# Weight residuals of thirteen units: ScalarE and an accumulating transfer in place of a VectorE subtraction

## The chip, the cores and the metric

One core of a Trainium2 chip runs the kernel. The metric is the device time of one execution in microseconds (us), and less is better. The engines named below are TensorE (PE in the profile), VectorE (DVE), ScalarE (ACT), GpSimd (POOL) and SyncE (SP), which here only issues transfers. TensorE's clock has two levels, 1.2 and 2.4 GHz; the profile gives the granted clock as a share of the upper one.

## What is computed

A decoder trunk of two layers over 512 tokens of width 1024, in float32. Each layer normalizes its input, multiplies it by one combined matrix, and splits the columns among two mixers: a diagonal state space model (S5) and a gated linear attention (GLA). Their outputs go through one output matrix and are added to the input; then a SwiGLU feed-forward block is added.

```python
for i in range(DEPTH):
    z = rmsnorm(x, norm_mix[i]) @ w_in[i]          # u | q | k | v | g | gate
    y = gelu(s5(u)); y = y * sigmoid(y @ w_glu[i] + b_glu[i])
    x = x + concat([rmsnorm(y), gla(q, k, v, g, gate)]) @ w_out[i]
    gu = rmsnorm(x, norm_ffn[i]) @ w_ffn_in[i]
    x = x + (silu(gu[..., :D_FF]) * gu[..., D_FF:]) @ w_ffn_out[i]
return rmsnorm(x, norm_final)
```

## The kernel before, in words

Activations lie transposed, features on the 128 partitions and the 512 tokens along the free axis. Each large matrix product is made three times to keep float32 accuracy: weights and activations are both split into a rounded part (`hi`, type float32r) and the residual that rounding leaves (`lo`), and `mm3` (L575 to L578) adds up hi times hi, hi times lo and lo times hi. L576 and L577 need only the rounded weights (`whi`), L578 needs the residuals (`wlo`).

The weights are cut into 128x128 blocks in the order in which they are used, and eight blocks make a unit of 512 KB (`UB = 8`). The first layer's units are: 0 to 3 the columns u, 4 to 7 q, k, q, k, 8 to 10 three tiles of g, 11 to 14 the columns v, 15 the last tile of g, 16 and 17 the `glu` matrix, 18 and on the output matrix and the feed-forward block. The class `Weights` brings them in:

- `load` (L142) has SyncE issue the transfer of one unit from HBM into a `raw` tile. There are two `raw` buffers, so the load of unit v+2 waits until nothing reads raw unit v any more.
- `ensure` (L155 to L168) prepares units up to two ahead of the one in use. For each it issues the next load, has ScalarE round raw into `whi` (L163), and has VectorE subtract, raw minus `whi`, into `wlo` (L165); unit 17's subtraction is made by GpSimd instead (`POOL_W`). There are three buffers each of `whi` and `wlo`, so the rounding of unit v waits for TensorE to be done with unit v-3.

What sets the order: TensorE, ScalarE and SyncE work in the order in which the program is written (`manual_schedule`), and so does VectorE in the first layer up to unit 10. GpSimd's order, and VectorE's elsewhere, is written by a planner ahead of the run from times that it assumes; the subtraction has high priority in it. Every engine then works strictly through its queue, so an instruction that waits holds all that is behind it.

Beside the products of units 3 to 15 the first layer also prepares its S5 mixer. `prep_w` builds the matrix `Wk`: VectorE transposes 128x512 tiles (L441), and for each of eight tiles SyncE issues four small transfers into `Wk` (`place`, L446), in the same queue as the loads of raw weights. `prep_v` and `prep_rot` build `Vx`, `Tz`, `cosT` and `sinT` on GpSimd (L407 to L417, L567 to L572). Then, for each of four groups b, `s5_fwd(b)` multiplies U by `Wk` (L833), VectorE rotates (L841 to L844), GpSimd adds (L846, L847), VectorE scans (L852); `s5_back(b)` rotates back on VectorE and GpSimd (L866 to L874); `s5_y(b)` is TensorE's product of the result (L888, L890) and ScalarE's gelu (L899). These calls are spread over the products of v by `v_tiles`. After them come `y_split` (L583, L584), the last tile of g (L992, L1001) and `glu`.

Of the kernel before, what the change touches and what calls it, by code (L numbers as in the profile page):

```python
# [10 lines left out]
F32 = mybir.dt.float32  # L11
# [3 lines left out]
ALU = mybir.AluOpType  # L15
# [24 lines left out]
GLU_MID = 1  # L40
NORM_AT = 3
RF_AT = 4
POOL_W = (17,)
FF_PARTS = (3, 4, 5, 5, 5)

O_Q, O_K, O_V, O_G, O_R = 512, 768, 1024, 1536, 2048
# [81 lines left out]
class Weights:  # L128
# [27 lines left out]
    def ensure(self, u):  # L156
        while self.next_split <= min(u + self.LOOK, DEPTH * NUNIT - 1):
            v = self.next_split
            self.load(v + 1)
            raw = self.raw.pop(v)  # L160
            hi = self.pool.tile([P, UB * P], F32R, tag="whi", name=f"whi{v}", bufs=3)
            lo = self.pool.tile([P, UB * P], F32R, tag="wlo", name=f"wlo{v}", bufs=3)
            self.nc.scalar.copy(hi, raw)  # L163
            with self.tc.high_priority():
                (self.nc.gpsimd if v in POOL_W else self.nc.vector).tensor_tensor(lo, raw, hi.bitcast(F32), op=ALU.subtract)  # L165
            self.split[v] = (hi, lo)
            self.next_split += 1
            self.split.pop(v - 6, None)  # L168
# [1341 lines left out]
```

## Time and profile before

| | |
|---|---|
| median of three runs | 1160.06 us (1159.01 to 1160.10) |
| the profiled execution | 1159.86 us |
| its span, first to last instruction | 1158.1 us |
| mean granted TensorE clock | 0.987 |
| TensorE busy | 1110.1 us, 96% of the span |
| VectorE busy | 706.2 us, 61% |
| ScalarE busy | 485.6 us, 42% |
| GpSimd busy | 331.9 us, 29% |
| the rounding L163 | 183 times, 1050 ns each |
| VectorE's subtraction L165 | 182 times, 1333 ns each |
| load of a raw unit | 183 times, 512 KB, 3.5 us to landing (median) |

The shares are means over the whole span. Over most of it, the feed-forward blocks and the second layer, TensorE has hardly a gap. The units that the change touches are used in the first 190 us, and that stretch is read by itself, from tables of ten microseconds each, the engines' own timelines and the waits.

### The profile page before, as it was taken

The numbers are of one execution on the slowest core, as the hardware profiler recorded it, in microseconds if no ns is written. First come the engines' busy times: TensorE is split into PE (matmuls) and PEld (weight loads), VectorE is DVE, ScalarE is ACT, GpSimd is POOL, SyncE is SP. The second block draws the span as 40 slices with busy tenths as digits, with TensorE's granted clock in tenths as the row PEclk, the third lists the DMA queues.
The fourth block names the chain that finished last, engine by engine and source line by source line (L and its number), as shares of the span: only waits on it lengthen the run. The fifth ranks groups of instructions, "written<-read, shape, count | busy, mean of one in ns | idle before, by whom it ended". The sixth has DMA issues, their size and how long they took to land.

```text
span 1158.1 us, 13973 instructions
## 1 busy us (share of the span) xinstructions
PE 1110.1 (96%) x5316; PEld 913.9 (79%) x5316; DVE 706.2 (61%) x947; ACT 485.6 (42%) x844; POOL 331.9 (29%) x322
## 2 busy tenths in 40 slices
PE   8789779999999999999999799999999999999997
PEld 5568658888888888888887688888888888888886
DVE  7996976866454454564466994686545444444454
ACT  6853458443232232432358653745323222222243
POOL 6899544546000052065030440352000000000003
PEclk9899889999999999999999999999999999999999
DMA  6155111244343523232331212123332333223221
GB/s 211 55 112 126 37 37 37 92 130 116 103 109 100 137 91 101 82 109 91 93 104 41 73 61 85 56 91 94 107 100 85 106 99 102 91 91 109 91 91 73
DMA packets 64099, 107.72 MB, mean 93 GB/s; under 512 B 37408, under 2 KB 38304, under 8 KB 64032
## 3 DMA queue, kind: packets, MB, share of 16 engines
q1 hardware_dynamic: 63888, 106.56, 30.2%
q8 instruction: 42, 0.69, 0.2%
q10 hardware_dynamic: 144, 0.26, 0.1%
q14 instruction: 25, 0.20, 0.1%
HBM read 100.52 MB, written 2.10 MB: 89 GB/s over the span
## 4 chain that ended last, share of the span: by engine, by line
PE 79%; DVE 12%; ACT 3%; issue 2%; POOL 2%; DMA 1%; SPq 1%; DVEq 0%; POOLq 0%; ACTq 0%
PE fg L576 7%; PE fg L577 7%; PE fg L578 7%; PE fu L578 7%; PE fu L576 7%; PE fu L577 7%; PE fo L578 7%; PE fo L576 7%; PE fo L577 7%; DVE ro L852 2%; DVE wlo L165 2%; ACT U L745 1%; DVE qz L814 1%; DMA wrr<-in_wr_dram 1%; DMA raw<-in_wst_dram 1%
## 5 line engine op out<-in xcount | busy, mean ns | idle before, releaser
L165 DVE TENSOR_TENSOR wlo<-raw,whi 128x1024 fp32r<-128x1024 f32 x182 | 242.2, 1333 | 113.2 <-ACT whi L163 112.0
L163 ACT CAST whi<-raw 128x1024 fp32r<-128x1024 f32 x183 | 191.8, 1050 | 280.0 <-PE fo L577 116.9
L602 POOL TENSOR_TENSOR sq_fin<-sq_fin 128x512 f32<-128x512 f32 x5 | 6.5, 1296 | 341.8 <-ACT sq_fin L598 341.8
L1237 DVE TENSOR_TENSOR fu<-fu,rs_ffn 128x512 f32<-128x512 f32 x44 | 30.4, 691 | 116.7 <-PE fu L578 113.9
L1254 DVE TENSOR_TENSOR xall<-xall,fo 128x512 f32<-128x512 f32 x78 | 53.1, 686 | 61.9 <-PE fo L578 61.7
L1234 DVE TENSOR_TENSOR fg<-fg,rs_ffn 128x512 f32<-128x512 f32 x44 | 30.3, 688 | 34.7 <-PE fg L578 30.8
L1236 ACT ACTIVATE fg<-fg 128x512 f32<-128x512 f32 x44 | 27.7, 629 | 42.5 <-DVE fg L1234 42.4
L899 ACT ACTIVATE y<-y 32x128 f32<-32x128 f32 x128 | 34.4, 269 | 20.9 <-PE y L890 17.3
L1238 DVE TENSOR_TENSOR fu<-fg,fu 128x512 f32<-128x512 f32 x44 | 31.3, 711 | 5.7 <-ACT fg L1236 1.3
L745 ACT COPY U<-u 32x128 f32<-32x128 f32 x128 | 32.9, 257 | 1.5
L852 DVE TENSOR_TENSOR_SCAN ro<-sp_mag,ro 128x128 f32<-128x128 f32 x64 | 28.5, 507 | 6.6 <-POOL ro L846 6.6
L1089 POOL TENSOR_TENSOR xall<-xall,wo 128x512 f32<-128x512 f32 x16 | 25.5, 1613 | 24.0 <-DVE wo L1088 24.0
L407 POOL TENSOR_TENSOR pt<-bc,sp_a1r 128x256 f32<-128x256 f32 x2 | 1.7, 852 | 94.0 <-issue 92.0
L568 POOL TENSOR_TENSOR rt<-rg 128x512 f32<-128x512 f32 x8 | 10.2, 1288 | 59.8 <-ACT rg L548 59.7
L602 POOL TENSOR_TENSOR sq_s<-sq_s,sq_s 128x512 f32<-128x512 f32 x6 | 8.1, 1342 | 64.3 <-ACT sq_s L598 64.3
L869 POOL TENSOR_TENSOR sr<-ro,ro 128x508 f32<-128x508 f32 x8 | 14.6, 1826 | 39.3 <-DVE ro L867 39.3
L602 POOL TENSOR_TENSOR sq_x1nmix<-sq_x1nmix 128x512 f32<-128x512 f32 x7 | 9.2, 1315 | 57.3 <-ACT sq_x1nmix L598 57.3
L890 PE MATMUL y<-sr,Vx 128*128 128x128 f32 x64 | 15.0, 322 | 8.0 <-POOL sr L869 7.8
L890 PE MATMUL y<-sm,Vx 128*128 128x128 f32 x64 | 14.8, 318 | 6.2 <-POOL sm L874 6.2
L888 PE MATMUL y<-U,Tz 128*128 128x128 f32 x64 | 14.9, 320 | 5.5 <-DVE ro L842 5.4
L846 POOL TENSOR_TENSOR ro<-ro,ro 128x512 f32<-128x512 f32 x8 | 10.7, 1344 | 30.8 <-DVE ro L843 30.8
L890 PEld LDWEIGHTS y<-sr,Vx 128*128 128x128 f32 x64 | 11.9, 231 | 8.9 <-POOL sr L869 8.9
(1257 smaller groups left out, 3533.0 us busy)
## 6 DMA issues: line engine op xcount, KB each, us to landing
raw<-in_wst_dram SPq DMA_DIRECT2D x183, 512.0 KB, 3.5
Wk<-wt SPq DMA_DIRECT2D x64, 64.0 KB, 3.9
xall<-in_xt_dram SPq DMA_DIRECT2D x3, 512.0 KB, 8.5
out_dram<-fin SPq DMA_DIRECT2D x6, 256.0 KB, 2.2
bc<-in_s5bc_dram SPq DMA_DIRECT2D x4, 256.0 KB, 4.1
raw<-in_wst_dram SPq DMA_DIRECT2D x1, 384.0 KB, 5.8
cst<-in_const_dram SPq DMA_DIRECT2D x1, 384.0 KB, 5.0
xall<-in_xt_dram SPq DMA_DIRECT2D x1, 283.0 KB, 3.0
```

The source lines that it names most:

```text
L163: self.nc.scalar.copy(hi, raw)
L165: (self.nc.gpsimd if v in POOL_W else self.nc.vector).tensor_tensor(lo, raw, hi.bitcast(F32), op=ALU.subtract)
L576: nc.tensor.matmul(ps, whi, xh, start=start, stop=False)
L577: nc.tensor.matmul(ps, whi, xl, start=False, stop=False)
L578: nc.tensor.matmul(ps, wlo, xh, start=False, stop=stop)
L745: nc.scalar.copy(u[32 * t:32 * t + 32, j].rearrange("p (n c) -> p n c", n=NCH), pv[32 * j:32 * j + 32, :, t, :],)
L852: v.tensor_tensor_scan(dst[:, cs], sp["mag4"][:, c:c + 1].to_broadcast([P, P]), src[:, cs], 0.0, M, A)
L890: nc.tensor.matmul(o, Vx[:, pr, part, 1:].rearrange("p a b c -> p (a b c)"), s_[:, cs], start=False, stop=(part == 1),)
L899: nc.scalar.activation(yv[32 * j:32 * j + 32, :, t, :], ps[32 * t:32 * t + 32, j * P:(j + 1) * P].rearrange("p (n c) -> p n c", n=NCH), AF ...
L1237: nc.vector.tensor_tensor(u, pu, rstd[0], op=M)
L1238: nc.vector.tensor_tensor(u, g, u, op=M)
L1254: nc.vector.tensor_tensor(xT[n], xT[n], ps[n], op=A)
```

## The change

For the first layer's units 5 to 17, ScalarE writes the negated rounded weights into `wlo` with a second instruction, and then GpSimd issues a transfer from `raw` to `wlo` that adds what it carries to what is there, so that `wlo` ends as raw minus hi. The subtraction on VectorE (units 5 to 16) and on GpSimd (unit 17) is gone. The transfer has the high priority that the subtraction had. All other units stay as they were.

```diff
-POOL_W = (17,)
+POOL_W = ()
+DMA_W = range(5, 18)
...
             self.nc.scalar.copy(hi, raw)
-            with self.tc.high_priority():
-                (self.nc.gpsimd if v in POOL_W else self.nc.vector).tensor_tensor(lo, raw, hi.bitcast(F32), op=ALU.subtract)
+            if v in DMA_W:
+                self.nc.scalar.mul(lo, hi.bitcast(F32), -1.0)
+                with self.tc.high_priority():
+                    self.nc.gpsimd.dma_start(lo.bitcast(F32), raw, accum_op=ALU.add)
+            else:
+                with self.tc.high_priority():
+                    (self.nc.gpsimd if v in POOL_W else self.nc.vector).tensor_tensor(lo, raw, hi.bitcast(F32), op=ALU.subtract)
             self.split[v] = (hi, lo)
```

## Rows read from the trace of the kernel before

**Rows 1.** Table by stage: stretch, length, busy us (instructions) by engine, clock, DMA, GB/s.

```profile
10.00:20.00 10.00, 8.56 (x35) 6.03 (x35) 9.49 (x8) 6.97 (x13) 5.86 (x4) 1.00 0.89 312
...
50.00:60.00 10.00, 9.45 (x42) 7.49 (x40) 9.86 (x10) 9.77 (x25) 9.85 (x12) 1.00 0.25 96
...
80.00:90.00 10.00, 10.00 (x48) 8.29 (x47) 9.89 (x12) 2.10 (x2) 9.71 (x9) 1.00 0.82 161
90.00:100.00 10.00, 10.00 (x51) 8.33 (x50) 5.84 (x8) 3.94 (x6) 10.00 (x8) 1.00 1.01 226
...
120.00:130.00 10.00, 4.97 (x21) 4.70 (x22) 9.80 (x20) 2.75 (x4) 7.08 (x8) 0.67 0.17 52
```

**Rows 2.** TensorE's timeline: start us, length us, what [idle before <-releaser].

```profile
62.38 0.79 PE L578 MATMUL q<-x0h,wlo 128*128 128x512 f32 x1 [2.93 <-DVE wlo L165]
...
71.14 0.50 PE L578 MATMUL k<-x0h,wlo 128*128 128x512 f32 x1 [1.68 <-DVE wlo L165]
...
101.47 1.13 PE L833 MATMUL x<-U,Wk 128*128 128x128 f32 x8 [1.00 <-DMA Wk<-wt]
...
118.30 0.39 PE L915 MATMUL v<-whi,x5l 128*128 128x512 f32 x1
...
124.07 0.76 PE L888 MATMUL y<-U,Tz 128*128 128x128 f32 x2 [5.38 <-DVE ro L842]
...
130.41 1.95 PE L833 MATMUL x<-U,Wk 128*128 128x128 f32 x16
```

**Rows 3.** Rounding and subtraction, 0 to 250 us: duration ns min/median/max, first and last start.

```profile
L163 ACT CAST whi<-raw x30: 1029/1046/1077, 10.7 to 246.9; 128x1024 fp32r<-128x1024 f32 x30
...
L165 DVE TENSOR_TENSOR wlo<-raw,whi x29: 1176/1314/2136, 11.8 to 248.2; 128x1024 fp32r<-128x1024 f32 x29
...
L165 POOL TENSOR_TENSOR wlo<-raw,whi x1: 2382/2382/2382, 160.2 to 160.2; 128x1024 fp32r<-128x1024 f32 x1
```

**Rows 4.** ScalarE's timeline: the roundings of units 6 and 7.

```profile
55.53 1.05 ACT L163 CAST whi<-raw 128x1024 fp32r<-128x1024 f32 x1
...
67.03 1.05 ACT L163 CAST whi<-raw 128x1024 fp32r<-128x1024 f32 x1
```

**Rows 5.** SyncE's timeline: issues of raw loads and of transfers into Wk.

```profile
67.36 4.08 SPq L142 DMA_DIRECT2D raw<-in_wst_dram  x2
...
96.01 2.71 SPq L446 DMA_DIRECT2D Wk<-wt  x4
```

**Rows 6.** Issues of raw loads, 55 to 105 us, and their time to landing.

```profile
L142 SPq DMA_DIRECT2D raw<-in_wst_dram x8: 333/560/1301, 67.4 to 99.3; - x8
...
DMA to landing us min/median/max: 3.5/4.3/5.2
```

**Rows 7.** Time to landing of all raw loads of the run.

```profile
DMA to landing us min/median/max: 2.8/3.5/7.7
```

**Rows 8.** GpSimd's timeline.

```profile
83.88 1.24 POOL L567 TENSOR_TENSOR cosT<-rk 128x512 f32<-128x512 f32 x1
85.08 2.04 POOL L570 TENSOR_TENSOR sinT<-rg,rk 128x512 f32<-128x512 f32 x1
...
112.49 1.29 POOL L846 TENSOR_TENSOR ro<-ro,ro 128x512 f32<-128x512 f32 x1
...
160.16 2.38 POOL L165 TENSOR_TENSOR wlo<-raw,whi 128x1024 fp32r<-128x1024 f32 x1
```

**Rows 9.** VectorE's timeline.

```profile
84.87 1.33 DVE L165 TENSOR_TENSOR wlo<-raw,whi 128x1024 fp32r<-128x1024 f32 x1
...
133.96 1.21 DVE L165 TENSOR_TENSOR wlo<-raw,whi 128x1024 fp32r<-128x1024 f32 x1
135.20 0.69 DVE L841 TENSOR_TENSOR ro<-x,cosT 128x512 f32<-128x512 f32 x1
...
160.24 2.85 DVE L584 TENSOR_TENSOR yg01l<-y,yg01h 128x512 fp32r<-128x512 f32 x1
```

**Rows 10.** Waits between 40 and 190 us: who for whom, us in total, times, longest.

```profile
PE gl L576 <- ACT yg03h L583: 3.0, 1, 3.0
```

## The prediction

> **What bounds the kernel now.** Read the table by stage first, and of it only the first 190 us; after that TensorE runs without a gap, so what the change gains or loses on the way to there arrives at the end one for one. From 50 us on VectorE and GpSimd are both busy for some 99% of the time [rows 1]. VectorE has less to do from 90 us; GpSimd stays full to about 118 us. The DMA engines are busy for 0.82 and 1.01 of 80 to 100 us [rows 1], mostly with the small transfers into Wk. Next, TensorE's timeline shows what is late. Twice it stands before a residual: 2.93 us for unit 6 and 1.68 us for unit 7 [rows 2]. At 101.47 it stands for Wk, and from 118.7, when v's sixth step ends, it stands 5.38 us for the first S5 product [rows 2]. After that wait the granted clock of the stretch is 0.67 [rows 1]: the product and its surroundings take from 124.07 to 130.41, where the lower level of 1.2 GHz, in place of 2.4, costs about half. The S5 group that TensorE waits for hung on GpSimd: L846 starts at 112.49, behind the preparation [rows 8], and VectorE's scans come after it. So three things end last in turn: VectorE's queue (to 80 us), GpSimd's preparation (to 118 us), and the exchange of VectorE and GpSimd (to 165 us).
>
> **What is removed.** Twelve subtractions on VectorE, 1.31 us each [rows 3], 15.8 us; and one of 2.38 us on GpSimd. Those of units 6 to 14 (nine) lie beside GpSimd's preparation and slow it: L570 took 2.04 us beside the subtraction of 84.87, L567, of the same shape, 1.24 just before [rows 8, 9]. At 0.8 us each GpSimd would get back up to 7 us; I take 4, since other VectorE instructions move into the place of some. Units 15 and 16 lie in the exchange, where VectorE's next instruction comes directly behind (133.96 to 135.20) [rows 9]; without them the exchange is 2 x 1.2 = 2.4 us shorter. Unit 17's subtraction on GpSimd, 160.16 to 162.54 [rows 8], lies beside VectorE's L584, which took 2.85 us [rows 9], though the same shape takes about 0.7 elsewhere on that engine (L841 [rows 9]). That L584 stands ahead of the last g tile, the last gelu and y3's split, for which TensorE waits 3.0 us [rows 10]. So 2.85 - 0.7 = 2.1 us come back there, and this I count as gained in every case.
>
> **What is added on ScalarE.** A second instruction of the rounding's shape, 1.05 us [rows 3], per unit. ScalarE is full from 40 to 67 us (9.77 of 10 us in 50:60 [rows 1]), so the negations of units 5 and 6 delay the work behind them, the roundings of later units included. Unit 6 is rounded at 55.53 + 1.05 = 56.6 and negated by 58.7; unit 7 is rounded at 67.03 + 2.1 = 69.1 and negated by 71.2 [rows 4]. Later ScalarE waits for loads, and the negation lengthens that path alone.
>
> **What is added on GpSimd, the queue and the buffer.** No row of this run shows a transfer issued by GpSimd or an adding one, so its price D, from the end of the negation to the residual in place, is bounded. It has three parts. Waiting for GpSimd's running instruction: 0 to a whole one of 1.24 us [rows 8], half of it, 0.6, taken. Issuing: between SyncE's shortest issue in this stretch, 0.33 us [rows 6], and GpSimd's whole 128x1024 subtraction, 2.4 us [rows 8]; I take 1.0, nearer to the issue, since no elements are computed. Moving: a raw load of the same 512 KB lands in 4.3 us here [rows 6], between 2.8 and 7.7 over the run [rows 7]. At 312 GB/s and 0.89 busy [rows 1] the engines would move 350 GB/s, so 0.524 MB are 1.5 us of their time. The adding transfer reads two tiles, so I take 4.3 + 1.5 = 5.8 us. A gain from D itself is excluded: a transfer can't land before it is issued. Sum D = 0.6 + 1.0 + 5.8 = 7.4; low end 0 + 0.3 + 2.8 = 3.1; high end 1.2 + 2.4 + 7.7 = 11.3.
>
> D matters because raw is held until the transfer has landed. SyncE's load of unit v+2 waits for it, and behind that load in SyncE's queue are the transfers into Wk, which alternate with the loads [rows 5]. The negations of units 6 and 7 end at 58.7 and 71.2, so their residuals are there at 66.1 and 78.6, where TensorE had them at 62.4 and 71.1 [rows 2]. From then on a round is load 4.3, rounding and negating 2.1, D 7.4, some 14 us for two units; TensorE's own work for two units is 11 (24 products of 0.227 us each). By the odd units: load 9 at 78.7, residual 9 at 92.5, residual 11 at 106.4. By the even ones: load 8 at 67.4 [rows 5], residual 8 at 81.1, load 10 at 81.8 (behind four Wk transfers that waited behind load 9), residual 10 at 95.6, load 12 at 95.8, residual 12 at 109.6, load 14 at 109.8. The last four Wk transfers start at 110.4 where they started at 96.01 [rows 5]: 14.4 us late, three times D and a constant.
>
> **What of that reaches the end.** TensorE's wait at 101.47 ends at 115.9, and it comes to the first S5 product at 118.7 + 14.4 = 133.1 in place of 124.07: 9.0 us late. It comes there straight from work, so the product runs at the upper level and takes about half of 6.3 us, 3.1 less; against that, it now stops some 4 us for Wk (v's first step, held by residual 11 until 106.4, ends 5.5 later), which by the 3.1 us that the stop of 5.4 cost in its wake I put at 2 us of lower level behind it. The third group's input (130.41 before [rows 2]) starts 9.0 - 3.1 + 2.0 = 7.9 us late, at 138.3, and ends at 140.2, where VectorE took it up at 135.2 [rows 9]: 5.0 us late. VectorE itself, which has lost the subtractions of 15 and 16, would have been there earlier. From there the exchange runs as before, 5.0 late. GpSimd's nine issues (9 x 1.0 - 4 = 5 us later at L846, 117.5) stay under it: 117.5 - 112.5 - 2.4 = 2.6. Together 5.0 - 2.1 = **+2.9 us**. By one us of D this moves by 3 in the range in which the round trip is the bound, which ends at about D = 5.5 below.
>
> On the profiled execution (1159.86, 1.76 us more than its span) that is 1162.8; on the median of the runs, 0.2 us higher, **1163.0**. About 0.2%, 2.3 us, is what a measurement of this kernel can tell from no change.
>
> **Rivals.** (a) *The transfer is quick and VectorE's relief wins.* For it: SBUF to SBUF has no HBM in its way, and the shortest load lands in 2.8 us [rows 7]. Below D of some 5.5 Wk is late by less than TensorE's stop at 124 covers, and the exchange is 2.4 us shorter, the split 2.1: up to -4.5, 1155.6; at D = 5.5 some -2.8. Middle 1156.5. Against it: the DMA engines are full at 80 to 100 us [rows 1], and eight more transfers of two reads each, 3 us of engine time each, come into that stretch. The Trainium skill's page "DMA: Bandwidth & Descriptors", section "Anatomy of one DMA — SWDGE (gpsimd) path", puts such a transfer at 2.0 us plus its bytes at 436 GB/s; an estimate by it is 3.2 us for one tile, D would be near 4 to 5, and the time about this rival's. No run here shows that figure yet.
>
> (b) *GpSimd becomes the bound by its order.* Its queue was written ahead; a transfer placed there waits for a negation that waits for a load that waits for an earlier transfer, and cosT, sinT, Tz and L846 stand behind it. That GpSimd has no gap between 46 and 118 us now (9.85, 9.71 and 10.00 us of 10 [rows 1]) is the case for it: each stop goes to L846. It decides once stops and issues together exceed the 5 us that I have counted by more than 2; nine transfers at 2 us each would be 18 - 4 = 14 late at L846, less 2.4 and 2.1: +9.5, **1169.6**. Against it: with the priority that it has the planner puts it where it believes the negation done.
>
> (c) *All is hidden.* Wk and the residual are late by just what the stop at 124 and the quicker exchange give back: within 2 us, 1160.
>
> That the change doesn't do what it says would be VectorE still making twelve subtractions; nothing points to it.
>
> **How the numbers follow.** Forecast (D of 6 to 9, -1.3 to +7.7) 0.40, of it 0.14 within 0.2%, 0.24 slower, 0.02 faster; (a) 0.28, of it 0.26 faster; (b) 0.20, slower; (c) 0.12, same. Sums: faster 0.28, same 0.28, slower 0.44. The range leaves out 0.1 on either side: below at the quick end of (a), 1155.5; above at D near 11.3, +2.9 + 3 x 3.9 = +14.6, and most of (b): 1174.7. The likeliest case's own range is 1158.8 to 1167.8.
>
> **What would show it.** In the profile after, each step has its row: L163's line with two ScalarE instructions per unit of 1.05 us; the waits of L578 on a transfer in units 6 and 7, ending near 66 and 79; the last Wk issue near 110; TensorE's stop at the first S5 input ending near 116 and no stop at the first S5 product; L584 of yg01 at 0.7. If the last Wk issue is before 100, D was under 5 and (a) holds. If GpSimd shows idle time before its transfers and L846 starts past 120 while Wk has long landed, (b) holds. The forecast is wrong if D is out of 6 to 9, or if GpSimd's issue is above 1.5 us.

## The result, and the profile after

The changed kernel takes **1167.85 us** (median of three runs, 1166.86 to 1168.48) against 1160.06: a ratio of 1.0069 (95% interval 1.0046 to 1.0092), some 8 us slower. The profiled execution is the one of 1167.85; its span is 1165.9 us (1158.1 before) and the mean granted clock 0.979 (0.987 before). VectorE's busy time fell from 706.2 to 685.6 us, ScalarE's rose from 485.6 to 499.2. In the changed file all lines behind the edit stand six lower: the rounding is L164, the negation L166, the adding transfer L168, the subtraction L171, and x, the S5 input, is L839 (L833 before).

The first view is TensorE's timeline of the changed kernel, as in [rows 2]: start us, length us, what, [idle before <-releaser].

```profile
67.69 0.79 PE L584 MATMUL q<-x0h,wlo 128*128 128x512 f32 x1 [8.52 <-DMA wlo<-raw]
...
80.38 0.80 PE L584 MATMUL k<-x0h,wlo 128*128 128x512 f32 x1 [4.75 <-DMA wlo<-raw]
...
106.64 0.50 PE L920 MATMUL v<-wlo,x0h 128*128 128x512 f32 x1 [0.87 <-DMA wlo<-raw]
...
114.58 1.13 PE L839 MATMUL x<-U,Wk 128*128 128x128 f32 x8 [2.39 <-DMA Wk<-wt]
...
120.45 2.04 PE L839 MATMUL x<-U,Wk 128*128 128x128 f32 x8 [4.74 <-DMA Wk<-wt]
...
138.97 0.38 PE L894 MATMUL y<-U,Tz 128*128 128x128 f32 x2
...
141.65 1.95 PE L839 MATMUL x<-U,Wk 128*128 128x128 f32 x16
...
177.79 0.50 PE L582 MATMUL gl<-yg03h,whi 128*128 128x512 f32 x1 [2.30 <-ACT yg03h L589]
```

The stops for residuals 6, 7 and 11 end at 67.69, 80.38 and 106.64. The stop for Wk ends at 120.45, where it ended at 101.47 before [rows 2]: 19.0 us later. The first S5 product is reached without a stop, as forecast, but at 138.97. The last row, gl, the output of the last g tile, started at 170.22 before; it starts 7.6 us later now, nearly the whole loss.

The table by stage (columns as in [rows 1]) tells why Wk is late.

```profile
80.00:90.00 10.00, 9.62 (x31) 7.75 (x32) 1.66 (x3) 3.30 (x4) 9.13 (x11) 0.70 1.11 222
90.00:100.00 10.00, 10.00 (x48) 8.31 (x47) 2.27 (x5) 3.54 (x4) 8.77 (x10) 1.00 0.84 169
100.00:110.00 10.00, 9.13 (x43) 7.26 (x42) 4.89 (x6) 3.23 (x5) 5.98 (x6) 1.00 0.92 175
110.00:120.00 10.00, 3.32 (x18) 2.46 (x16) 1.29 (x2) 5.19 (x6) 4.75 (x6) 0.84 1.02 219
```

VectorE, full before at 80 to 90 us [rows 1], is now busy for 1.66 of these 10 us and nearly idle at 110 to 120. The DMA engines had shares of 0.82 and 1.01 to 100 us [rows 1], and 0.32 and 0.01 in the two stretches behind that (the last but one number of each row), here from the kernel before:

```profile
100.00:110.00 10.00, 9.00 (x101) 7.55 (x100) 8.58 (x11) 3.49 (x7) 10.00 (x9) 1.00 0.32 107
110.00:120.00 10.00, 8.69 (x57) 6.88 (x55) 6.12 (x8) 4.14 (x9) 7.75 (x9) 1.00 0.01 2
```

Now the shares are 0.84 to 1.11 as far as 120 us. The share adds up the times of packets; that it passes 1 shows that these can overlap. From the page of the changed kernel, the queue of the adding transfers (packets, MB, share of 16 engines' span), and the issues (KB each, median us to landing):

```profile
q0 software_dynamic: 1872, 6.82, 3.3%
...
raw<-in_wst_dram SPq DMA_DIRECT2D x183, 512.0 KB, 3.5
wlo<-raw POOLq DMA_DIRECT2D x13, 512.0 KB, 5.2
Wk<-wt SPq DMA_DIRECT2D x64, 64.0 KB, 4.0
```

By this count one adding transfer takes 0.033 x 1165.9 / 13 = 3.0 us of all 16 engines. (In the kernels further down with transfers for late units alone, where the engines have little else to do, it is 2.9 to 3.1, so the crowd did not lengthen it.) Six of them are issued between 80 and 120 us, the last at 119.31: 18 us of full load. SyncE's timeline shows what that does to its issues:

```profile
67.98 12.75 SPq L143 DMA_DIRECT2D raw<-in_wst_dram  x2
80.82 3.47 SPq L452 DMA_DIRECT2D Wk<-wt  x4
...
92.99 5.18 SPq L452 DMA_DIRECT2D Wk<-wt  x4
...
107.08 4.87 SPq L452 DMA_DIRECT2D Wk<-wt  x4
112.07 0.55 SPq L143 DMA_DIRECT2D raw<-in_wst_dram  x1
113.13 2.72 SPq L452 DMA_DIRECT2D Wk<-wt  x4
```

Before, each such group of four took 2.6 to 2.7 us at this place, as the 2.71 of [rows 5]; now up to 5.18. The last group starts at 113.13 in place of 96.01. And SyncE's waits between 60 and 125 us (us in total, times, longest) show the held buffers:

```profile
SPq L143 <- DMA wlo<-raw: 31.3, 6, 11.8
```

Before, in the same 65 us, the loads waited 10.9 us in three stops for VectorE's subtraction.

Last, VectorE's timeline, which carries the lateness on:

```profile
122.61 0.69 DVE L849 TENSOR_TENSOR ro<-x,sinT 128x512 f32<-128x512 f32 x1 [5.50 <-PE x L839]
...
126.15 2.22 DVE L858 TENSOR_TENSOR_SCAN ro<-sp_mag,ro 128x128 f32<-128x128 f32 x4
...
144.33 0.69 DVE L847 TENSOR_TENSOR ro<-x,cosT 128x512 f32<-128x512 f32 x1
...
169.99 0.69 DVE L590 TENSOR_TENSOR yg01l<-y,yg01h 128x512 fp32r<-128x512 f32 x1
```

The third group's rotation starts at 144.33, 135.20 before [rows 9]: 9.1 us late. The split of yg01 takes 0.69 in place of 2.85 [rows 9].

### The profile page after: what moved, and what is told of

Same layout as the page of the kernel before. It is cut to its first block, busy times and chain, and to the rows that moved or that the text cites. A ratio compares the mean times of both kernels' runs of the same rounds, so it can differ in the third digit from the quotient of the medians.

```text
span 1165.9 us, 14005 instructions
## 1 busy us (share of the span) xinstructions
PE 1112.1 (95%) x5316; PEld 916.5 (79%) x5316; DVE 685.6 (59%) x935; ACT 499.2 (43%) x857; POOL 328.2 (28%) x334
## 4 chain that ended last, share of the span: by engine, by line
PE 78%; DVE 3%; ACT 3%; issue 0%; DVEq 0%; ACTq 0%
PE fg L582 7%; PE fg L583 7%; PE fu L582 7%; PE fu L583 7%; PE fg L584 7%; PE fu L584 7%; PE fo L582 7%; PE fo L583 7%; PE fo L584 7%; ACT U L751 1%; PE v L919 1%; PE gl L583 1%; PE gl L582 1%; PE wo0s L584 1%; PE wo1s L584 1%; PE wo1s L583 1%
## 5 line engine op out<-in xcount | busy, mean ns | idle before, releaser
L164 ACT CAST whi<-raw 128x1024 fp32r<-128x1024 f32 x183 | 191.8, 1050 | 299.6 <-PE fo L583 114.8
L171 DVE TENSOR_TENSOR wlo<-raw,whi 128x1024 fp32r<-128x1024 f32 x170 | 225.5, 1329 | 108.3 <-ACT whi L164 107.0
L839 PE MATMUL x<-U,Wk 128*128 128x128 f32 x128 | 17.2, 289 | 7.1 <-DMA Wk<-wt 7.1
L839 PEld LDWEIGHTS x<-U,Wk 128*128 128x128 f32 x128 | 16.5, 205 | 7.9 <-issue 7.7
L852 POOL TENSOR_TENSOR ro<-ro,ro 128x512 f32<-128x512 f32 x8 | 11.1, 1381 | 31.3 <-DVE ro L849 31.3
```

Of the source, the lines that this page charges most:

```text
L839: nc.tensor.matmul(ps[part][:, j * P:(j + 1) * P], Wk[:, part, 4 * b + j], U[b][:, j], start=True, stop=True,)
```

## The experiments

Each ratio is against runs of the kernel before on the same chip (medians 1159.5 to 1160.0), with a 95% interval.

### The parts of the change

**ScalarE's part alone.** The negation is kept; in place of the transfer VectorE (GpSimd for unit 17) adds raw to it.

```diff
-                    self.nc.gpsimd.dma_start(lo.bitcast(F32), raw, accum_op=ALU.add)
+                    (self.nc.gpsimd if v == 17 else self.nc.vector).tensor_tensor(lo, raw, lo.bitcast(F32), op=ALU.add)
```

> ScalarE's part alone: for units 5 to 17 ScalarE writes the negated rounded weights, and VectorE (GpSimd for unit 17) adds raw to them as before; no transfer is issued by GpSimd. Theory, the time that a transfer holds the raw buffer: this costs little, the two negations before 67 us put the work behind them 2.1 us later, so 1160 to 1162.5 us. Rival, ScalarE's longer path is the cause: most of the 7.8 us stays, 1165 to 1168.

Measured: 1162.3 us, 1.0022 [1.0013, 1.0031]. The second ScalarE instruction costs about 2.6 us where nothing else is gained by it. TensorE has no stop for Wk here, and the table of 80 to 120 us has the DMA engines 0.82, 0.91, 0.27 and 0.16 busy.

**Early units alone, late units alone.**

```diff
-POOL_W = ()
-DMA_W = range(5, 18)
+POOL_W = (17,)
+DMA_W = range(5, 15)
```

> Transfers for units 5 to 14 only; 15 and 16 are subtracted by VectorE and 17 by GpSimd as before the change. Theory, the round trip of the raw buffer ahead of the transfers into Wk: all of the loss is in these units and the gains of the late ones are missing, so the changed kernel's 1167.9 plus about 4.5 (2.4 in the exchange, 2.1 at the split): 1170 to 1173. Rival, late units cost as much as early ones: at or below the changed kernel's time, 1163 to 1167.

```diff
-DMA_W = range(5, 18)
+DMA_W = (15, 16, 17)
```

> Transfers for units 15 to 17 only; 5 to 14 are subtracted by VectorE. Theory: no early loss, and the gain of the late units shows, 2.4 us in the exchange of VectorE and GpSimd and 2.1 us at the split: 1155.6 to 1157.7. Rival, an adding transfer costs wherever it stands (its issue in GpSimd's queue beside the exchange): 1160 to 1163.

Measured: early units alone 1170.79, 1.0099 [1.0085, 1.0113]; late units alone 1157.72, 0.9982 [0.9973, 0.9991]. The two add up to +9.1 us, where both together cost 7.8. All of the loss belongs to units 5 to 14, the ones whose transfers run beside those into Wk. With the early units alone (GpSimd still subtracts for unit 17) TensorE's, VectorE's and GpSimd's timelines have:

```profile
119.67 2.04 PE L839 MATMUL x<-U,Wk 128*128 128x128 f32 x8 [2.43 <-DMA Wk<-wt]
```

```profile
173.25 2.86 DVE L590 TENSOR_TENSOR yg01l<-y,yg01h 128x512 fp32r<-128x512 f32 x1
```

```profile
173.20 2.35 POOL L171 TENSOR_TENSOR wlo<-raw,whi 128x1024 fp32r<-128x1024 f32 x1
```

Wk is late by 18.2 us, as after the whole change, and the split of yg01 is long again, since GpSimd's subtraction lies beside it. That settles why this split was long: with that subtraction beside it 2.85 and 2.86, without it 0.69. (The 2.16 us between them are called the split gain below; what of it arrives at the end is another matter, see the versions with late units.) The late units alone gained 2.0 us, about the split gain; the shorter exchange that I had looked for gave little: the third group's rotation starts 0.9 earlier, not 2.4.

### What makes Wk late

Three suspects: the late issue on GpSimd of the first transfers, the held raw buffers, and the load on the DMA engines.

**The late issue.** GpSimd's timeline after the change:

```profile
62.90 0.88 POOL L168 DMA_DIRECT2D wlo<-raw  x1
75.76 0.88 POOL L168 DMA_DIRECT2D wlo<-raw  x1
...
115.25 0.88 POOL L168 DMA_DIRECT2D wlo<-raw  x1 [6.45 <-ACT wlo L166]
...
123.38 1.27 POOL L852 TENSOR_TENSOR ro<-ro,ro 128x512 f32<-128x512 f32 x1 [0.51 <-DVE ro L849]
```

Units 6 and 7 were negated by 58.6 and 71.1; their transfers stand 4.3 and 4.6 us in GpSimd's order. Leaving units 6 and 7 on VectorE takes this away:

```diff
-DMA_W = range(5, 18)
+DMA_W = (5,) + tuple(range(8, 18))
```

> The changed kernel, but VectorE subtracts units 6 and 7 as before the change; transfers for 5 and 8 to 17. It takes away the two long stops of TensorE (8.5 and 4.75 us), which came from GpSimd taking up those two transfers 4.3 and 4.6 us after the negation. Theory, the load on the DMA engines (full from 80 to 120 us): ten of thirteen transfers still meet the transfers into Wk, the last of which land near 110 us or later: 1162 to 1166. Rival, the late issue of 6 and 7 in GpSimd's order starts the whole delay: 1156.5 to 1160.

Measured: 1165.75, 1.0054 [1.0039, 1.0069]. Of some 8 us, 2 are gone, 6 stay. The two intervals overlap, but the trace agrees, with a stop for Wk that ends 2.0 us earlier. Wk still comes late:

```profile
118.50 2.05 PE L839 MATMUL x<-U,Wk 128*128 128x128 f32 x8 [5.56 <-DMA Wk<-wt]
```

**The held buffers.** A third raw buffer lets the load of unit v+2 start while raw unit v is still being carried; two activation buffers are given up to make room.

```diff
-            t = self.pool.tile([P, UB * P], F32, tag="raw", name=f"raw{u}", bufs=2)
+            t = self.pool.tile([P, UB * P], F32, tag="raw", name=f"raw{u}", bufs=3)
...
-    NACT = 45
+    NACT = 43
```

> The changed kernel with three raw buffers in place of two, and 43 in place of 45 activation buffers, which makes the room. A load then no longer waits for the transfer two units before it. Theory, the hold of the raw buffer: the loads and the transfers into Wk behind them leave early again (last Wk issue near 100 us), the stop for Wk is gone, the two stops for the residuals of units 6 and 7 stay: 1158 to 1162. Rival, GpSimd's queue (its waits for negations, L852 late) or the DMA engines' load: 1165 to 1168.

The control is the same edit of the kernel before.

> The kernel before with three raw buffers and 43 activation buffers: what the raw3 edit does by itself. Theory: without the adding transfers loads hardly wait for raw, so it costs and brings nothing, 1158.5 to 1161. Rival: two activation buffers fewer hold work up (ScalarE's gelu of the third S5 group waited for a buffer in the changed kernel with three raw buffers), 1162 to 1165, and that kernel has then to be read against this one.

Measured: 1168.29, 1.0073 [1.0059, 1.0087], for the changed kernel; 1163.9, 1.0036 [1.0022, 1.0050], for the control. So both theories missed: the buffer does not bring the time back, and it costs 3.9 us by itself. Between the two the change is worth 1.0073 / 1.0036 = 1.0037 (by the two intervals, taken as independent, 1.0017 to 1.0057), +4.4 us in place of +7.8. The rows say more than the sum: with the third buffer the changed kernel has

```profile
114.84 2.05 PE L839 MATMUL x<-U,Wk 128*128 128x128 f32 x8 [2.82 <-DMA Wk<-wt]
```

```profile
167.12 0.69 DVE L590 TENSOR_TENSOR yg00l<-y,yg00h 128x512 fp32r<-128x512 f32 x1 [5.18 <-ACT yg00h L589]
```

So the stop for Wk ends 5.6 us earlier than with two buffers, but still 13.4 later than before the change. Yet the third buffer takes away most of the waiting: up to the last Wk issue SyncE's loads stand 5.9 us for adding transfers, where they stood 20.9 with two buffers. So holding raw is a part of Wk's lateness, and by this pair of runs not the larger. The time does not follow the 5.6, because at the split of yg00 VectorE now waits 5.18 us for ScalarE (2.60 with two buffers; in the control 2.78, before 1.25). ScalarE itself stands 4.89 us for TensorE's y and 4.59 for VectorE's rp ahead of it (1.06 and 3.87 with two buffers). Whether the two activation buffers fewer are behind that is not shown.

**The bytes.** The transfer carries one block of eight, 64 KB in place of 512; the other seven blocks' residuals stay unfinished, minus hi, so this kernel only serves to read the time. All issues and waits remain.

```diff
-                    self.nc.gpsimd.dma_start(lo.bitcast(F32), raw, accum_op=ALU.add)
+                    self.nc.gpsimd.dma_start(lo[:, 0:P].bitcast(F32), raw[:, 0:P], accum_op=ALU.add)
```

> The changed kernel, but each adding transfer carries only the first 128 of 1024 columns (64 KB in place of 512), so the residuals of the other seven blocks are left unfinished; all instructions, their queues and waits stay. Theory, the load on the DMA engines: loads and transfers into Wk land after some 3.5 to 4 us again, the last Wk issue comes near 103 us and the stop for Wk ends near 107: 1157 to 1161. Rival, GpSimd's order, its waits and ScalarE's longer path: 1164 to 1168.

Measured: 1159.6, 0.9999 [0.9990, 1.0009]: without the bytes the loss is gone. The stop for Wk and the third rotation:

```profile
111.76 1.13 PE L839 MATMUL x<-U,Wk 128*128 128x128 f32 x8 [2.52 <-DMA Wk<-wt]
```

```profile
135.39 0.69 DVE L847 TENSOR_TENSOR ro<-x,cosT 128x512 f32<-128x512 f32 x1
```

Wk is still 10.3 us late (4.8 later than expected), and VectorE takes up the third group at 135.39, 0.2 later than before: that much lateness is covered. The edit shortens the holding too (a transfer lands in 2.4 us in place of 5.2, medians), so by itself it does not tell bytes on the engines from time in the buffer. But the waits for held buffers are still there: up to the last Wk issue SyncE's loads stand 22.3 us for transfers, 20.9 in the changed kernel. So these waits are enough for some 10 us of lateness, and with them alone nothing is lost against the kernel before. Against the late units alone (0.9982) some 2 us are; the 2.6 that ScalarE's negations cost by themselves would cover them.

**The load alone.** To the kernel before, with all its subtractions, a copy of 1 MB from HBM to a scratch tensor in HBM is added for each of units 5 to 17, issued by ScalarE. It touches no raw buffer and is not in GpSimd's queue; nothing waits for it.

```diff
+            if 5 <= v < 18:
+                self.nc.scalar.dma_start(self.junk[2 * v - 10:2 * v - 8], self.src[2 * v:2 * v + 2])
```

> The kernel before, with the load of the thirteen transfers but nobody waiting for it: behind the rounding of each unit from 5 to 17 ScalarE issues a plain copy of 1 MB from HBM to HBM, about the 3.0 us of all DMA engines' time that one adding transfer took; the subtractions stay. Theory, the time for which each transfer holds raw and the residual: the load by itself delays loads and the transfers into Wk by some us only, 1160 to 1163. Rival, the DMA engines' load is what costs: 1165 to 1169.

The control copies 64 KB each.

> The run load_only again (1169.2 us), with 64 KB per copy in place of 1 MB: the same issues on ScalarE, a sixteenth of the load. Theory, the load on the DMA engines: the transfers into Wk and the loads land and are issued as in the kernel before, 1159 to 1161.5. Rival, the issues in ScalarE's queue or the changed order of the planner cost by themselves: 1164 or more.

In the run with 1 MB the theory missed and its rival held; the theory of the control held. Measured: 1169.17, 1.0086 [1.0062, 1.0111], with the 1 MB copies (1165.06 to 1174.12 over four runs, the profiled one 1165.06); 1159.56, 0.9999 [0.9990, 1.0009], with the small ones. The page of the 1 MB kernel, the queue of the copies, and two stretches of its TensorE's and SyncE's timelines:

```profile
q10 hardware_dynamic: 560, 13.89, 3.5%
```

```profile
111.71 2.04 PE L836 MATMUL x<-U,Wk 128*128 128x128 f32 x8 [11.31 <-DMA Wk<-wt]
114.27 2.04 PE L836 MATMUL x<-U,Wk 128*128 128x128 f32 x8 [0.52 <-DMA Wk<-wt]
```

```profile
86.47 6.10 SPq L449 DMA_DIRECT2D Wk<-wt  x4
```

A copy takes (3.5% - 0.1%) x 1163 / 13 = 3.0 us of all engines (0.1% is that queue's share without the copies), as much as an adding transfer, and the load by itself makes Wk 12.8 us late and the kernel slower by as much as the change did. The issues as such cost nothing. That the copies also load HBM, which the adding transfer does not, is a difference that this run leaves.

The Trainium skill's page "DMA: Bandwidth & Descriptors", section "Issuing engines are not separate DMA queues", says that transfers from any engine end on the same 16 engines and interleave there. This pair of runs agrees: copies that ScalarE issues make SyncE's transfers late, with a stop for Wk that ends 12.8 us later. The same section calls the time to start a transfer usually small beside the transfer. In this row four starts took 6.10 us, 1.5 each, beside a median of 5.5 to landing for the Wk transfers of 60 to 130 us; that is not small.

### Versions that keep the late units only

Unit 14 added to the late units; unit 17 given to VectorE; and, without any transfer, only unit 17's subtraction moved from GpSimd to VectorE (`POOL_W = ()` in the kernel before).

```diff
-DMA_W = range(5, 18)
+DMA_W = (14, 15, 16, 17)
```

> Transfers for units 14 to 17. Against units 15 to 17 alone (1157.7), unit 14's subtraction, 2.0 us at 105 us beside GpSimd's preparation, goes too, and its transfer falls behind the last transfers into Wk. Theory: GpSimd's preparation, which the scans wait for, gets some tenths of a us back and the residual is in time: 1156.5 to 1157.7. Rival: the transfer holds raw 14 and GpSimd's queue in a full stretch: 1158 to 1160.

```diff
-DMA_W = range(5, 18)
+DMA_W = (15, 16)
```

> Transfers for units 15 and 16; unit 17 is subtracted by VectorE in place of GpSimd. Theory: the gain at the split comes from GpSimd's subtraction being away from beside VectorE's, not from the transfer; unit 17's negation (1.05 us ahead of the third gelu on ScalarE) is saved: 1156.5 to 1158. Rival, the transfer of 17 is what gains: 1159 to 1160.5.

> The kernel before with unit 17's subtraction on VectorE in place of GpSimd; no transfer and no negation anywhere. Theory: it takes away only what slowed VectorE's L584 of yg01 to 2.85 us, and adds 1.2 us to VectorE ahead of it while it waits for ScalarE: 1157.5 to 1159. Rival: the slow L584 was hidden, 1159.5 to 1160.5.

Measured, in this order: 1156.76, 0.9976 [0.9967, 0.9985]; 1157.88, 0.9982 [0.9973, 0.9991]; 1158.27, 0.9992 [0.9983, 1.0001]. The first is faster than both kernels, by 0.24% against the one before. In its TensorE's timeline the stop for Wk is where it was before the change:

```profile
100.75 1.13 PE L839 MATMUL x<-U,Wk 128*128 128x128 f32 x8 [0.72 <-DMA Wk<-wt]
...
166.90 0.49 PE L582 MATMUL gl<-yg03h,whi 128*128 128x512 f32 x1 [2.46 <-ACT yg03h L589]
```

How much of these gains needs the transfer stays open. The transfer of unit 17 gains nothing of its own: with the unit given to VectorE the ratio is the same 0.9982 as for units 15 to 17. Without any transfer, moving unit 17 off GpSimd can't be told from no change; its median is 1.5 us lower, and its interval touches that of the first. In its trace the split of yg01 takes 0.68, and that of yg02 behind it starts 2.1 us earlier than before, but gl only 1.0: there the split gain arrives in part.

## Why the prediction came out as it did

The direction and the chain up to the stop for Wk were right: the round trip of the raw buffers, the Wk transfers behind the loads in SyncE's queue, the stop. The size was not: +2.9 us forecast, +7.8 measured, 0.05 us above the likeliest case's own range (1167.8) and inside the wide one. Step by step:

**ScalarE.** 1.05 us a negation forecast, 1.06 measured; units 6 and 7 negated by 58.6 and 71.1, forecast 58.7 and 71.2. Right. A reading beside it was too high: from 50 to 90 us GpSimd was busy for 96% (38.6 of 40 us), not some 99%; nothing in the sum hangs on it.

**D, the way from negation to residual.** The transfers between 60 and 125 us (L168: duration ns min/median/max; then us to landing, counted from the start of the issue):

```profile
L168 POOL DMA_DIRECT2D wlo<-raw x9: 851/876/1190, 62.9 to 119.3; - x9
...
DMA to landing us min/median/max: 4.6/5.8/7.4
```

Issue and landing were put at 1.0 + 5.8 = 6.8; they are 5.8 with the issue of 0.88 inside. The wait for GpSimd was put at 0.6; it was 4.3, 4.6 and 2.9 us for units 6 to 8, the early ones in GpSimd's order, and 0.3 to 0.9 for units 9 to 13, for all but one of which GpSimd stood waiting. Over units 6 to 13 D is 9.0, 9.2, 8.7, 4.9, 8.3, 7.1, 6.3 and 5.5: a mean of 7.4, as forecast, but by luck: two terms were off against each other. Residual 6 came at 67.7 (66.1 forecast), 7 at 80.4 (78.6), 9 at 92.5 (92.5), 11 at 106.6 (106.4).

The Trainium skill's page "DMA: Bandwidth & Descriptors", section "Anatomy of one DMA — SWDGE (gpsimd) path", by which the prediction worked out 3.2 us as an estimate, does not hold for the adding transfer here: 5.2 at the median over all thirteen, 4.5 at the least. For the transfer of 64 KB an estimate by the same fit is 2.0 + 0.15 = 2.2 us, and 2.4 was measured.

**The step that failed: the Wk transfers.** "14.4 us late, three times D and a constant." The constant left the issues of the Wk transfers (2.7 us for four) and their landing as they were in the trace of before. Beside the adding transfers neither stayed so. The last four start at 113.13, not 110.4: 1.8 us of the 2.7 because residual 7 came late, 0.9 because the four issues at 80.82 took 3.47 us (behind that, slower issues and a D of 8.3 us for unit 10 against one of 6.3 for unit 12 nearly cancel). From the last issue's end to TensorE's restart it is 120.45 - 115.85 = 4.6 us, where it was 101.47 - 98.72 = 2.75 in [rows 2, 5]. So the stop ends at 120.45, not at 115.9: 2.7 + 1.9 = 4.6 us, nearly the whole miss of 4.9. I had read 0.82 and 1.01 [rows 1] and used it only against rival (a); it belonged in the sum, with 3 us of full load for each transfer.

**From the stop to the end.** The prediction carried the lateness through TensorE, to 138.3 for the third group's input and 140.2 for VectorE. One term of that path was right: the first S5 product, reached from work, runs at the upper level of the clock (granted clock 1.00 from 138.97 to 141.65, where it was 0.52 from 124.07 to 130.41 before), and takes 2.68 us in place of 6.34, 3.7 less (3.1 forecast). But it starts at 138.97, not at 133.1, and the third group's input ends at 143.60, 0.7 before VectorE takes it up. The rows show VectorE as the carrier: it waits 5.50 us for x, and from 126.15 to 144.33 it stands once, for 0.84. Before, its first scan stood 4.61 us for GpSimd's L846:

```profile
113.81 4.54 DVE L852 TENSOR_TENSOR_SCAN ro<-sp_mag,ro 128x128 f32<-128x128 f32 x4 [4.61 <-POOL ro L846]
```

With that slack, and unit 14's subtraction of 2.00 us that stood ahead of it in VectorE's queue and is gone, the lateness falls from 19.0 at the stop to 12.3 at the first scan: 6.7 us are swallowed. From the first scan to the third rotation it took 21.4 us before and takes 18.2 now. That is 3.2 back, of which the two subtractions in that stretch, of 1.2 us each [rows 9], make 2.4. Then comes the split gain, 2.16. So 19.0 - 6.7 - 3.2 = 9.1 at the third rotation, 9.75 at the split of yg01, and 7.6 behind it. With the stop's end as it was forecast (14.4) this path gives 14.4 - 6.7 - 3.2 = 4.5 at the third rotation, against the 5.0 of the prediction. So taking the wrong carrier cost nothing in the sum, which is luck, and the miss goes back to Wk.

The same reading holds from run to run. Lateness in us against the kernel before (stop for Wk 101.47, first scan 113.81, third rotation 135.20, gl 170.22, profiled execution 1159.86):

| kernel | end of the stop for Wk | first scan | third rotation | gl | profiled execution |
|---|---|---|---|---|---|
| transfers of units 14 to 17 | -0.7 | -1.5 | -1.1 | -3.3 | -4.7 |
| transfers of 64 KB | +10.3 | +3.9 | +0.2 | -1.4 | -1.3 |
| copies of 1 MB, no change | +12.8 | +6.7 | +5.1 | +5.1 | +5.2 |
| third raw buffer, no change | no stop | +0.9 | +1.4 | +1.9 | +3.2 |
| third raw buffer and the change | +13.4 | +7.9 | +4.1 | +5.2 | +6.5 |
| units 6, 7 on VectorE | +17.0 | +10.7 | +6.9 | +5.4 | +5.9 |
| the change | +19.0 | +12.3 | +9.1 | +7.6 | +8.0 |
| early units alone | +18.2 | +12.7 | +13.1 | +13.0 | +13.3 |

With the late units' subtractions gone, some 10 us of lateness cost nothing, and beyond that nearly each microsecond counts. The third raw buffer loses on the way what it gains at Wk; 3.2 us of its loss are there without the change. The early units alone and the copies have neither the two subtractions out of the exchange nor the split gain.

**The rivals.** (a) fails: the transfer is not quick beside the others, and none of the thirteen landed below 4.5 us. (b) named its own sign, idle GpSimd and L846 (now L852) past 120 us with Wk long landed. GpSimd does wait, 11.2 us in four stops between 60 and 125 us, and L852 starts at 123.38. But it waits there for VectorE's L849, that for TensorE's x, and that for Wk, which let TensorE go at 120.45. GpSimd's order costs the 2 us that the run without units 6 and 7 gave back; it is not the bound. (c) fails for the change, with +7.8; it is what happens when the transfers carry little, at 0.9999.

**What stays open.** Load and holding are not told apart to the microsecond. At the stop for Wk the waits with hardly any load (64 KB, with all negations and GpSimd's order) make 10.3 us, the load without the waits (the copies) 12.8, the load with most of the waits taken away (third buffer) 13.4, and both together 19.0. The shares do not add up; a loaded engine also makes a buffer be held longer. What the load does is clear at the end all the same: the waits without it cost nothing against the kernel before, and it costs without them. Why the time of the kernel with the copies spreads over 9 us (1165.06 to 1174.12) is open too; the table shows its fastest run.

## What to carry to other kernels

An accumulating transfer in place of an elementwise instruction is not work taken away, it is work moved to the DMA engines and time added to the source buffer. Count its engine time, 3.0 us for 512 KB here, against the idle share of the very stretch where it will run, and look for what is queued behind the load that waits for its buffer. Where the DMA engines are mostly idle, as behind the last transfer into Wk, the same change of units 14 to 17 came with a small gain, 0.24%, and not all of that is shown to need the transfer.

## What the runs showed of the hardware

SyncE's issues themselves grow long beside another queue's transfers; it is not only the landing that gets later. Four transfers of 64 KB took 2.6 to 2.7 us to issue in 75 to 99 us of the kernel before. After the change the groups of four during which an adding transfer was under way took 3.47 to 5.18 us, and the one that met none (at 85.11) and the one that met only the start of one (at 113.13) took 2.66 and 2.72. The share of the DMA engines alone does not tell it: the 2.66 stand in a stretch with 1.11, and before the change 90 to 100 us had 1.01 with 2.67 and 2.71. Beside the copies of 1 MB a group took up to 6.10 us, but some took 2.71 to 3.33.

And an adding transfer from SBUF to SBUF takes no less of the DMA engines than a copy of twice its bytes from HBM to HBM: both 3.0 us.
